# Two weight sums of each FFN tile made by an adding DMA, and a new order of some FFN products

## The chip, the cores and the metric

The program runs on one core of one Trainium2 chip. The metric is device time in microseconds (us), lower is better; three runs of the kernel before gave 568.59, 568.89 and 569.35 us, so the time before is their median, 568.89 us.

## What is computed

One decoder layer over 512 tokens of width 1024 in float32: a norm, a mixer (attention, a state-space group, pooling), an output projection with a residual add, a norm, a SwiGLU FFN with 2816 hidden units, a residual add and a final norm. The change lies in the FFN:

```python
    x = x + jnp.concatenate([y_attn, y_ssd, y_pool], axis=-1) @ w_out
    h = rmsnorm(x, norm_ffn)
    gate, up = jnp.split(h @ w_gate_up, 2, axis=-1)
    return x + (jax.nn.silu(gate) * up) @ w_down
```

## The kernel before

Every float32 product is made of three matmuls: weights and activations are split into a high part in fp32r (a copy on ACT) and a low part (a subtraction on DVE), and `mm3` (L184) multiplies high by high, low by high and high by low.

The hidden units of the FFN are cut into 22 tiles of 128, in the groups `GROUPS` = (0, 4), (4, 8), (8, 12), (12, 16), (16, 18), (18, 22). Tile 0 (`PLAIN`) is multiplied plainly. For each of the other 21 tiles, gate and up of that tile are a 2 by 2 block product: two halves of the inner dimension (g1, g2 of the gate weights; v1, v2 of the up weights, 512 columns each in a tile of 128 x 1024) by two halves of the tokens (256 each). It is done with seven products instead of eight, P1 to P7, each of 4 x 3 matmuls of 256 columns. P1 and P2 take g1 and g2, P4 takes v2; P5, P6, P7 and P3 take the weight sums s1 = v1 + v2, s2 = s1 + g1, s3 = g1 + v1 and s4 = s2 + g2. P4 to P7 multiply sums of the activations, T1 to T4, which DVE makes once at the start of the FFN (`h2_sums`). P1, P6, P7 and P4 follow one another in one PSUM bank, `psB`; ACT copies its running value to a tile `u` after P1, P6 and P7 (L1107), before the next product may add to it. P5 and P3 share `psC`, P2 has `psA`.

The weights come by `load_ahead` (L879): a list of 512 KB loads on SP's queue into `NRAW` = 4 buffers; r_g is a tile's gate, r_u its up, r_d a piece of w_down. The work on them is a list of steps per tile, `plan`: `split_g`, `add_up` (all four sums, on DVE, into two tiles `sa`, `sb` with two buffers in all), `split_v`, and `split_s` twice, for sa = (s1, s2) and for sb = (s3, s4). A step is taken by `advance` whenever buffers of the split weights are free and its load should have landed, in the course of the products; a scheduler then fixes each engine's order. An engine takes its instructions in that order, and waits at the first whose operands are not there.

`pair_order` writes down the products of a group: two tiles overlap, so that PE has other work while ACT copies `psB`. The last two products of a group's last tile, P4 and P3, are its tail; they stand behind the first block of the group's down products (`pd`), four banks of 512 tokens each, added by DVE to the residual x1 (`add_x1`, L797). The tiles 1 to 3 (`EARLY`) have P1 and P2 ahead of all (`FIRST`), since the sums T come late. At that time, the start of the FFN, the loads of x1, of the gate weights of tiles 1 to 3 and the last split of w_out (half of it on GpSimd, POOL in the profile) fall together.

```python
            s_, q_ = sums[i] = [sp.tile([P, 1024], F32, name=f"{n}{i}", tag="s") for n in ("sa", "sb")]
            nc.vector.tensor_tensor(s_[:, :512], v1, v2, ALU.add)
            nc.vector.tensor_tensor(s_[:, 512:], s_[:, :512], g1, ALU.add)
            nc.vector.tensor_tensor(q_[:, :512], g1, v1, ALU.add)
            nc.vector.tensor_tensor(q_[:, 512:], s_[:, 512:], g2, ALU.add)
```

Of the kernel before, what the change touches and what calls it, by code (L numbers as in the profile page):

```python
# [114 lines left out]

def layer(tc, xT, xn, w1, wz, wv, wo, wgu, wd, par, poolw, gffn, gfin, out):
    nc = tc.nc
    L = Lanes()
    ctx = ExitStack()
    with ctx:  # L120
# [740 lines left out]
        def all_loads():  # L861
            for lo_, hi_ in GROUPS:
                order = [(w, i) for i in range(lo_, hi_) for w in "gu"]
                if lo_ == 0:
                    first = [(w, i) for i in PLAIN for w in "gu"] + [("g", i) for i in EARLY]
                    order = first + [q for q in order if q not in first]
                for w, i in order:
                    yield (w, i), wgu[2 * i + (w == "u")]
                for h in range(2):
                    for kp in range(lo_ // 2, hi_ // 2):  # L870
                        yield ("d", kp, h), wd[2 * kp + h]

# [6 lines left out]
        def load_ahead():  # L879
            while len(raws) < NRAW:  # L880
                key, src = next(loads, (None, None))
                if key is None:
                    return
                raws[key] = rawp.tile([P, 1024], F32, name="r_" + "_".join(map(str, key)), tag="raw")
                nc.sync.dma_start(raws[key], src)
                dma_free[0] = max(dma_free[0], L.clock) + 1.6
                landed[key] = dma_free[0] + 2.5

        def used(*keys):
            for key in keys:  # L890
# [12 lines left out]
        def add_up(i):  # L903
            load_ahead()
            r0, r1 = raws["g", i], raws["u", i]
            g1, g2, v1, v2 = r0[:, :512], r0[:, 512:], r1[:, :512], r1[:, 512:]
            s_, q_ = sums[i] = [sp.tile([P, 1024], F32, name=f"{n}{i}", tag="s") for n in ("sa", "sb")]
            nc.vector.tensor_tensor(s_[:, :512], v1, v2, ALU.add)
            nc.vector.tensor_tensor(s_[:, 512:], s_[:, :512], g1, ALU.add)  # L909
            nc.vector.tensor_tensor(q_[:, :512], g1, v1, ALU.add)  # L910
            nc.vector.tensor_tensor(q_[:, 512:], s_[:, 512:], g2, ALU.add)
            used(("g", i))

# [13 lines left out]
        def split_s(i, m):  # L927
            kind = ("wx", "w")[m]
            h_, l_ = slot(kind, f"sh{m}{i}"), slot(kind, f"sl{m}{i}")
            hi_lo(sums[i][m], h_, l_, nc.vector)  # L930
            for k_, n in enumerate(((5, 6), (7, 3))[m]):
                ops[i, n] = (h_[:, k_ * 512 : (k_ + 1) * 512], l_[:, k_ * 512 : (k_ + 1) * 512])

        def split_d(kp, h):
# [194 lines left out]
        def block(i, n):  # L1129
# [9 lines left out]
            for kt in range(4):  # L1139
                sl = slice(kt * P, (kt + 1) * P)  # L1140
                mm3(ps, w_hi[:, sl], w_lo[:, sl], *moving(n, kt), new and kt == 0, kt == 3, chain=not new)
            if n in (2, 5, 3):
                done("w" if n == 3 else "wx", 2)
            elif n == 4:
                done("wx", 1)
# [34 lines left out]
        def pair_order(lo_, hi_):  # L1180


            tiles = [i for i in range(lo_, hi_) if i not in PLAIN]
            order = []
            for i, nxt in zip(tiles, tiles[1:] + [None]):
                if (i, 6) not in order:
                    order += [(i, n) for n in (1, 2, 6, 5, 7) if (i, n) not in order and (i, n) not in FIRST]
                if nxt is None:
                    return order, [(i, 4), (i, 3)]
                if nxt in EARLY:  # L1190
                    order += [(nxt, 6), (i, 4), (nxt, 5), (i, 3), (nxt, 7)]
                else:
                    order += [(nxt, 1), (i, 4), (nxt, 2), (i, 3)]

        for gi, (lo_, hi_) in enumerate(GROUPS):
# [21 lines left out]
            for h in range(2):  # L1217
                last = gi == len(GROUPS) - 1 and h == 1
                kps = range(lo_ // 2, hi_ // 2)
                if not last:  # L1220
                    pss = [bank(f"pd{gi}{h}_{t}") for t in range(NT)]
                    for kp in kps:
                        w_hi, w_lo = need(("d", kp, h))
                        for j in range(2):
                            k = 2 * kp + j
                            js = slice(j * 512, (j + 1) * 512)
                            if h == 0 and k == lo_ + 1:
                                for q in tail:
                                    block(*q)
                            for t in range(NT):  # L1230
                                ts_ = slice(t * P, (t + 1) * P)
                                pd_end = mm3(pss[t], aT[k][0][:, ts_], aT[k][1][:, ts_], w_hi[:, js], w_lo[:, js], k == lo_, k == hi_ - 1)
                            advance()
# [52 lines left out]
def pack(inputs):  # L1286
# [64 lines left out]
```

## Time and profile before

| what | value |
|---|---|
| median of 3 runs | 568.89 us |
| the profiled execution, its own time | 569.56 us |
| its span | 567.9 us |
| PE matmuls | 556.4 us, 3504 of them |
| DVE, ACT, POOL busy | 432.2, 308.1, 30.7 us |
| moved by DMA | 61.62 MB, 109 GB/s on the mean |
| mean granted PE clock | 0.994 of full speed |

The span runs from the first to the last instruction; the execution's own time is 1.7 us longer. The FFN begins at about 213 us; the last of the output projection, the loads of x1 and the norm lie before it. In the rows below, PE is the matmul engine, SPq is SP's queue of DMA issues, and what stands in brackets behind a row is how long its engine stood idle before it and what ended that.

### The profile page before, as it was taken

How to read it: one execution, taken by the hardware profiler on the slowest of the kernel's cores; microseconds unless marked ns; L12 is line 12 of the kernel's file. 1: busy time of each engine (PE TensorE's matmuls, PEld its weight loads, DVE VectorE, ACT ScalarE, POOL GpSimd, SP SyncE). 2: the span in 40 equal slices, each digit the busy share in tenths (PEclk: the TensorE clock that was granted, in tenths of full speed). 3: DMA queues.
4: the chain of work that ended last, by engine and by line, in shares of the span. 5: the costliest groups of instructions: out<-in, count | busy, mean ns of one | idle time of the engine just before them, and what ended most of it. 6: DMA issues, size and time to landing. Idle time of an engine off the chain costs nothing.

```text
span 567.9 us, 9056 instructions
## 1 busy us (share of the span) xinstructions
PE 556.4 (98%) x3504; PEld 504.2 (89%) x3504; DVE 432.2 (76%) x788; ACT 308.1 (54%) x561; POOL 30.7 (5%) x47
## 2 busy tenths in 40 slices
PE   8999999999999999999999999999999999999995
PEld 4998998888987889998899989998999889899984
DVE  4479866898999678999967777776867876787346
ACT  5687645777767456655264524543255425345344
POOL 6001002006110000000000000000000000000000
PEclk8999999999999999999999999999999999999998
DMA  7962233322213601255232332343043233222004
GB/s 239 316 193 82 75 111 112 131 76 86 82 39 117 254 1 38 78 186 183 74 119 107 112 111 75 112 122 139 19 164 105 86 101 122 76 75 75 1 0 148
DMA packets 19663, 61.62 MB, mean 109 GB/s; under 512 B 2316, under 2 KB 3748, under 8 KB 19620
## 3 DMA queue, kind: packets, MB, share of 16 engines
q1 hardware_dynamic: 19044, 60.00, 31.3%
q10 hardware_dynamic: 576, 1.05, 0.5%
q8 instruction: 27, 0.44, 0.3%
q14 instruction: 16, 0.13, 0.1%
HBM read 58.93 MB, written 2.11 MB: 107 GB/s over the span
## 4 chain that ended last, share of the span: by engine, by line
PE 92%; DVE 4%; ACT 2%; DMA 1%; issue 1%; SPq 0%; ACTq 0%; DVEq 0%
PE psB L186 7%; PE psB L188 7%; PE psB L187 7%; PE pd L186 6%; PE pd L187 6%; PE pd L188 6%; PE pc L186 4%; PE pc L188 4%; PE pc L187 4%; PE psC L187 3%; PE psC L188 3%; PE psC L186 3%; PE po L186 2%; PE po L188 2%; PE po L187 2%; PE pn L186 2%
## 5 line engine op out<-in xcount | busy, mean ns | idle before, releaser
L187 PE MATMUL pd<-dl,aTh 128*128 128x512 f32 x160 | 62.4, 390 | 0.0
L186 PE MATMUL pd<-dh,aTh 128*128 128x512 f32 x160 | 61.6, 391 | 0.0
L188 PE MATMUL pd<-dh,aTl 128*128 128x512 f32 x160 | 58.6, 390 | 0.0
L157 DVE TENSOR_TENSOR wlo<-raw,whi 128x1024 fp32r<-128x1024 f32 (+3 forms) x29 | 34.3, 1181 | 14.3 <-ACT whi L156 13.1
L156 ACT ACTIVATE whi<-raw 128x1024 fp32r<-128x1024 f32 (+3 forms) x34 | 31.5, 930 | 23.5 <-PE pc L187 11.6
L858 ACT ACTIVATE sh<-sb 128x1024 fp32r<-128x1024 f32 x21 | 22.2, 1059 | 39.5 <-PE pd L187 18.5
L186 PE MATMUL pc<-hT_hi,whi 128*128 128x512 f32 x104 | 41.7, 401 | 0.0
L188 PE MATMUL pc<-hT_hi,wlo 128*128 128x512 f32 x104 | 40.8, 393 | 0.0
L1107 ACT COPY u<-psB 128x256 f32<-128x256 f32 x63 | 23.1, 366 | 32.6 <-PE psB L188 31.7
L187 PE MATMUL pc<-hT_lo,whi 128*128 128x512 f32 x104 | 40.7, 392 | 0.0
L858 ACT ACTIVATE dh<-r_d 128x1024 fp32r<-128x1024 f32 x22 | 23.3, 1060 | 26.3 <-PE psC L187 12.8
L859 DVE TENSOR_TENSOR gl<-r_g,gh 128x1024 fp32r<-128x1024 f32 x22 | 26.9, 1224 | 12.8 <-ACT gh L858 7.0
L186 PEld LDWEIGHTS pd<-dh,aTh 128*128 128x128 f32 x160 | 30.0, 188 | 6.2 <-ACT aTh L858 0.4
L188 PEld LDWEIGHTS pd<-dh,aTl 128*128 128x128 f32 x160 | 30.1, 188 | 6.1
L187 PEld LDWEIGHTS pd<-dl,aTh 128*128 128x128 f32 x160 | 30.1, 188 | 6.0
L859 DVE TENSOR_TENSOR sl<-sa,sh 128x1024 fp32r<-128x1024 f32 x21 | 25.7, 1223 | 11.6 <-PE psA L187 10.4
L858 ACT ACTIVATE gh<-r_g 128x1024 fp32r<-128x1024 f32 x22 | 23.3, 1058 | 20.0 <-DMA r_g<-wgu 10.8
L859 DVE TENSOR_TENSOR sl<-sb,sh 128x1024 fp32r<-128x1024 f32 x21 | 25.6, 1220 | 10.5 <-ACT sh L858 7.3
L859 DVE TENSOR_TENSOR dl<-r_d,dh 128x1024 fp32r<-128x1024 f32 x22 | 26.9, 1222 | 4.8 <-ACT dh L858 4.7
L797 DVE TENSOR_TENSOR x<-pd,x 128x512 f32<-128x512 f32 x44 | 27.9, 684 | 3.0 <-PE pd L188 3.0
L858 ACT ACTIVATE sh<-sa 128x1024 fp32r<-128x1024 f32 x21 | 22.3, 1060 | 14.3 <-DVE sa L909 7.9
L186 PE MATMUL po<-whi,mixT_hi 128*128 128x512 f32 x64 | 25.5, 401 | 0.0
(321 smaller groups left out, 1840.4 us busy)
## 6 DMA issues: line engine op xcount, KB each, us to landing
r_g<-wgu SPq DMA_DIRECT2D x22, 512.0 KB, 3.5
r_u<-wgu SPq DMA_DIRECT2D x22, 512.0 KB, 3.8
r_d<-wd SPq DMA_DIRECT2D x22, 512.0 KB, 3.6
raw<-w SPq DMA_DIRECT2D x13, 512.0 KB, 3.3
raw<-wo SPq DMA_DIRECT2D x8, 512.0 KB, 3.2
rawx<-xT SPq DMA_DIRECT2D x8, 256.0 KB, 3.4
rawn<-xn SPq DMA_DIRECT2D x4, 512.0 KB, 4.6
x<-xn SPq DMA_DIRECT2D x4, 512.0 KB, 7.3
```

Of the source, the lines that this page charges most:

```text
L156: nc.scalar.activation(hi[:, sl], raw[:, sl], AF.Copy)
L157: eng.tensor_tensor(lo[:, sl], raw[:, sl], hi[:, sl].bitcast(F32), ALU.subtract)
L186: nc.tensor.matmul(ps, s_hi, m_hi, start=first, stop=False, skip_group_check=chain)
L187: nc.tensor.matmul(ps, s_hi, m_lo, start=False, stop=False, skip_group_check=chain)
L188: last_mm = nc.tensor.matmul(ps, s_lo, m_hi, start=False, stop=last, skip_group_check=chain)
L797: nc.vector.tensor_tensor(x1[t][:, cs], ps, x1[t][:, cs], ALU.add)
L858: nc.scalar.activation(hi, src, AF.Copy)
L859: eng.tensor_tensor(lo, src, hi.bitcast(F32), ALU.subtract)
L1107: nc.scalar.copy(u_, e["B"])
```

## The change

The host packs a further array `wgs`: for each tile (v2, g1) and (v1, v1). SP loads the first into a tile `sa`; then GpSimd sends a DMA that adds the second to it on the way. So `sa` comes out as (s1, s3) with no DVE work. The two adds that are left, s2 and s4, are written over r_g's two halves, so r_g is kept until its second split. r_u loads only v2 (256 KB) where it was 512 KB. The two buffers of `sa` are asked for two tiles ahead: `sum_ahead` is called twice at the start and then after each split of an `sa`. P5 and P7 now have one split and P6 and P3 the other, and `pair_order` puts P5 ahead of P6. For the fifth group the tail is gone: P4 and P3 of tile 17 stand among P1 and P2 of tile 18. Where a group has a tail, its first down products are held until the last tile's latest product is issued.

```diff
@@ load_ahead, all_loads
                 for w, i in order:
-                    yield (w, i), wgu[2 * i + (w == "u")]
+                    half = w == "u" and i not in PLAIN
+                    yield (w, i), wgu[2 * i + (w == "u")][:, 512 * half :], 512 * half
...
-                nc.sync.dma_start(raws[key], src)
+                nc.sync.dma_start(raws[key][:, c0:], src)
...
+        sum_order = [i for i in range(FT) if i not in PLAIN]
+
+        def sum_ahead():
+
+            if sum_order:
+                i = sum_order.pop(0)
+                t_ = sums[i, 0] = sp.tile([P, 1024], F32, name=f"sa{i}", tag="sa")
+                nc.sync.dma_start(t_, wgs[2 * i])
+                nc.gpsimd.dma_start(t_, wgs[2 * i + 1], accum_op=ALU.add)
...
         def add_up(i):
             load_ahead()
-            r0, r1 = raws["g", i], raws["u", i]
-            g1, g2, v1, v2 = r0[:, :512], r0[:, 512:], r1[:, :512], r1[:, 512:]
-            s_, q_ = sums[i] = [sp.tile([P, 1024], F32, name=f"{n}{i}", tag="s") for n in ("sa", "sb")]
-            nc.vector.tensor_tensor(s_[:, :512], v1, v2, ALU.add)
-            nc.vector.tensor_tensor(s_[:, 512:], s_[:, :512], g1, ALU.add)
-            nc.vector.tensor_tensor(q_[:, :512], g1, v1, ALU.add)
-            nc.vector.tensor_tensor(q_[:, 512:], s_[:, 512:], g2, ALU.add)
-            used(("g", i))
+            r0, sa = raws["g", i], sums[i, 0]
+            sums[i, 1] = r0
+            nc.vector.tensor_tensor(r0[:, :512], sa[:, :512], r0[:, :512], ALU.add)
+            nc.vector.tensor_tensor(r0[:, 512:], r0[:, :512], r0[:, 512:], ALU.add)
...
-            hi_lo(sums[i][m], h_, l_, nc.vector)
-            for k_, n in enumerate(((5, 6), (7, 3))[m]):
+            hi_lo(sums.pop((i, m)), h_, l_, nc.vector)
+            for k_, n in enumerate(((5, 7), (6, 3))[m]):
                 ops[i, n] = (h_[:, k_ * 512 : (k_ + 1) * 512], l_[:, k_ * 512 : (k_ + 1) * 512])
+            if m == 0:
+                sum_ahead()
+            else:
+                used(("g", i))
...
         crit = []
+        for _ in range(2):
+            sum_ahead()
...
@@ block
-            if n in (2, 5, 3):
+            if n in (2, 7, 3):
                 done("w" if n == 3 else "wx", 2)
...
@@ pair_order
-                if (i, 6) not in order:
-                    order += [(i, n) for n in (1, 2, 6, 5, 7) if (i, n) not in order and (i, n) not in FIRST]
+                if (i, 5) not in order:
+                    order += [(i, n) for n in (1, 2, 5, 6, 7) if (i, n) not in order and (i, n) not in FIRST and (n > 2 or i not in st)]
+                if nxt is None and hi_ == 18:
+
+                    return order + [(hi_, 1), (i, 4), (hi_, 2), (i, 3)], []
                 if nxt is None:
                     return order, [(i, 4), (i, 3)]
                 if nxt in EARLY:
-                    order += [(nxt, 6), (i, 4), (nxt, 5), (i, 3), (nxt, 7)]
+                    order += [(nxt, 5), (i, 4), (nxt, 6), (i, 3), (nxt, 7)]
...
+                            hold = tc.issue_after(st[hi_ - 1]["end"]) if tail and h == 0 and k == lo_ else nullcontext()
+                            with hold:
+                                for t in range(NT):
+                                    ts_ = slice(t * P, (t + 1) * P)
+                                    pd_end = mm3(pss[t], aT[k][0][:, ts_], aT[k][1][:, ts_], w_hi[:, js], w_lo[:, js], k == lo_, k == hi_ - 1)
...
@@ pack
+    g_, v_ = wgu[0::2], wgu[1::2]
+    wgs = np.concatenate([v_[:, :, 512:], g_[:, :, :512], v_[:, :, :512], v_[:, :, :512]], axis=2)
+    wgs = np.ascontiguousarray(wgs.reshape(FT, P, 2, 1024).transpose(0, 2, 1, 3)).reshape(2 * FT, P, 1024)
```

How the instructions move is shown at three places. In the names the number behind a letter is the tile of the FFN, and the last four digits are a buffer's running number.

SP's queue at the start of the FFN, behind the loads of x1, before:

```order
L785 DMA x1_2_2050<-xn 128x1024
L785 DMA x1_3_2051<-xn 128x1024
L885 DMA r_g_1_2112<-wgu 128x1024
L885 DMA r_g_2_2114<-wgu 128x1024
L885 DMA r_g_3_2160<-wgu 128x1024
L885 DMA r_u_1_2172<-wgu 128x1024
L1241 DMA gf_5962<-gfin 128x1024
L885 DMA r_u_2_2610<-wgu 128x1024
L885 DMA r_u_3_2615<-wgu 128x1024
```

and now:

```order
L785 DMA x1_2_2050<-xn 128x1024
L785 DMA x1_3_2051<-xn 128x1024
L903 DMA sa1_2073<-wgs 128x1024
L903 DMA sa2_2076<-wgs 128x1024
L886 DMA r_g_1_2118<-wgu 128x1024
L886 DMA r_g_2_2120<-wgu 128x1024
L886 DMA r_g_3_2166<-wgu 128x1024
L886 DMA r_u_1_2178<-wgu 128x512
L1258 DMA gf_5941<-gfin 128x1024
L886 DMA r_u_2_2615<-wgu 128x512
L903 DMA sa3_2621<-wgs 128x1024
L886 DMA r_u_3_2641<-wgu 128x512
```

The loads of sa1 and sa2 have come in between x1 and the gates of tiles 1 to 3, and the one of sa3 between r_u of tiles 2 and 3. On POOL, the last instructions before (the split of w_out, `wlo30`, is the last but the end of the program):

```order
L703 MEMSET pwa1_1701 128x16
L703 MEMSET pwb1_1702 128x16
L487 TENSOR_TENSOR sz_219<-skp_238,sz_219 128x384 x2
L157 TENSOR_TENSOR wlo30_2093<-raw30_2091,whi30_2092 128x512
L1347 UNCONDITIONAL_BRANCH
L1347 ISA
```

and now, with the same split in the middle:

```order
L703 MEMSET pwb1_1702 128x16
L487 TENSOR_TENSOR sz_219<-skp_238,sz_219 128x384 x2
L904 DMA sa1_2073<-wgs 128x1024
L904 DMA sa2_2076<-wgs 128x1024
L157 TENSOR_TENSOR wlo30_2099<-raw30_2097,whi30_2098 128x512
L904 DMA sa3_2621<-wgs 128x1024
```

The adding DMAs of sa1 and sa2 stand ahead of `wlo30`, whose tile PE reads in the last products of the output projection. On DVE, the sums and splits of tile 1 (sh/sl are the high and low part of a pair of weight sums, the 0 or 1 ahead of the tile's number saying which split) before:

```order
L1024 TENSOR_TENSOR T1l_2322<-h2f10_2263,T1h_2321 128x4x128
L908 TENSOR_TENSOR sa1_2604<-r_u_1_2172 128x512
L910 TENSOR_TENSOR sb1_2605<-r_g_1_2112,r_u_1_2172 128x512
L859 TENSOR_TENSOR vh1_2612<-r_u_1_2172,vh1_2612 128x512
L1028 SCALAR_TENSOR_TENSOR h2f31_2431<-h2f10_2263,h2f31_2431 128x512
L1024 TENSOR_TENSOR T3l_2326<-h2f30_2422,T3h_2325 128x4x128
L909 TENSOR_TENSOR sa1_2604<-sa1_2604,r_g_1_2112 128x512
L1099 TENSOR_TENSOR g3_2541<-psA_3_2528,u1_3_2526 128x256
L1030 SCALAR_TENSOR_TENSOR h2f11_2272<-h2f31_2431,h2f11_2272 128x512
L1024 TENSOR_TENSOR T2l_2324<-h2f31_2431,T2h_2323 128x4x128
L911 TENSOR_TENSOR sb1_2605<-sa1_2604,r_g_1_2112 128x512
```

and now:

```order
L1036 TENSOR_TENSOR T1l_2328<-h2f10_2269,T1h_2327 128x4x128
L917 TENSOR_TENSOR r_g_1_2118<-sa1_2073,r_g_1_2118 128x512
L859 TENSOR_TENSOR vh1_2612<-r_u_1_2178,vh1_2612 128x512
L859 TENSOR_TENSOR sl01_2618<-sa1_2073,sh01_2617 128x1024
L917 TENSOR_TENSOR r_g_2_2120<-sa2_2076,r_g_2_2120 128x512
L1040 SCALAR_TENSOR_TENSOR h2f31_2437<-h2f10_2269,h2f31_2437 128x512
L1036 TENSOR_TENSOR T3l_2332<-h2f30_2428,T3h_2331 128x4x128
L918 TENSOR_TENSOR r_g_1_2118<-r_g_1_2118 128x512
```

The low part of tile 1's first split, `sl01`, stands three places behind T1's low part (T1l), where before ten instructions stood between them. On PE, the end of P7 of tile 17 (T3) and the start of its P4 (T4) before:

```order
L186 MATMUL psB_17_5176<-T3h_2325,sh117_5029 128x256
L187 MATMUL psB_17_5176<-T3l_2326,sh117_5029 128x256
L188 MATMUL psB_17_5176<-T3h_2325,sl117_5030 128x256
L186 MATMUL psB_17_5176<-T4h_2327,vh17_5003 128x256
L187 MATMUL psB_17_5176<-T4l_2328,vh17_5003 128x256
L188 MATMUL psB_17_5176<-T4h_2327,vh17_5003 128x256
```

and now the same end of P7:

```order
L186 MATMUL psB_17_5159<-T3h_2331,sh017_4993 128x256
L187 MATMUL psB_17_5159<-T3l_2332,sh017_4993 128x256
L188 MATMUL psB_17_5159<-T3h_2331,sl017_4994 128x256
L186 MATMUL psB_18_5290<-h2_hi_2079,gh18_5105 128x256
L187 MATMUL psB_18_5290<-h2_lo_2080,gh18_5105 128x256
L188 MATMUL psB_18_5290<-h2_hi_2079,gl18_5106 128x256
L186 MATMUL psB_18_5290<-h2_hi_2079,gh18_5105 128x256
```

P4 of tile 17 comes 21 matmuls later now, after the rest of P1 and all of P2 of tile 18.

## Rows read from the trace of the kernel before

**Rows 1.** Page, part 1: busy us of each engine, share of the span, instructions.

```profile
PE 556.4 (98%) x3504; PEld 504.2 (89%) x3504; DVE 432.2 (76%) x788; ACT 308.1 (54%) x561; POOL 30.7 (5%) x47
```

**Rows 2.** Windows: length, then PE, PEld, DVE, ACT, POOL busy; PEclk, DMA share, GB/s.

```profile
220.00:240.00 20.00, 19.93 (x167) 19.68 (x165) 19.41 (x32) 14.33 (x27) 0.00 (x0) 1.00 0.21 73
...
240.00:260.00 20.00, 19.24 (x140) 18.27 (x141) 19.08 (x29) 12.10 (x19) 0.00 (x0) 1.00 0.56 183
260.00:480.00 220.00, 220.00 (x1511) 205.63 (x1510) 166.95 (x246) 101.02 (x155) 0.00 (x0) 1.00 0.33 108
480.00:500.00 20.00, 19.36 (x117) 16.93 (x116) 15.37 (x25) 6.95 (x10) 0.00 (x0) 1.00 0.15 54
```

**Rows 3.** Timeline of PE, 235 to 249 us: start, length, instruction, idle before.

```profile
235.35 0.28 PE L186 MATMUL psB<-T2h,sh 128*128 128x256 f32 x1
...
239.53 0.28 PE L187 MATMUL psB<-T3l,sh 128*128 128x256 f32 x1
239.65 0.28 PE L188 MATMUL psB<-T3h,sl 128*128 128x256 f32 x1
240.76 0.39 PE L186 MATMUL psB<-T2h,sh 128*128 128x256 f32 x1 [0.83 <-ACT sh L858]
...
248.42 0.28 PE L187 MATMUL psC<-T1l,sh 128*128 128x256 f32 x1
248.69 0.39 PE L186 MATMUL psB<-T4h,vh 128*128 128x256 f32 x1
```

**Rows 4.** Timeline of PE, 483 to 499 us.

```profile
483.71 0.28 PE L188 MATMUL psB<-T3h,sl 128*128 128x256 f32 x1
484.45 0.39 PE L186 MATMUL psB<-T4h,vh 128*128 128x256 f32 x1 [0.46 <-ACT u L1107]
...
496.53 1.98 PE L188 MATMUL pd<-dh,aTl 128*128 128x512 f32 x8
498.68 0.39 PE L186 MATMUL psB<-h_hi,gh 128*128 128x256 f32 x1 [0.18 <-DVE x L797]
```

**Rows 5.** Timeline of DVE, 227 to 235 us; last, the groups of instructions of ACT.

```profile
227.93 0.69 DVE L908 TENSOR_TENSOR sa<-r_u 128x512 f32<-128x512 f32 x1
...
234.25 1.23 DVE L859 TENSOR_TENSOR sl<-sa,sh 128x1024 fp32r<-128x1024 f32 x1 [0.49 <-ACT sh L858]
...
L858 ACT ACTIVATE sh<-sa 128x1024 fp32r<-128x1024 f32 x21 | 22.3, 1060 | 14.3 <-DVE sa L909 7.9 <-PE psB L188 6.4
```

**Rows 6.** DMA issues: xcount, KB, median us to landing; last, tile x, 176 to 200 us.

```profile
r_g<-wgu SPq DMA_DIRECT2D x22, 512.0 KB, 3.5
out<-x SPq DMA_DIRECT2D x2, 128.0 KB, 2.0
...
DMA to landing us min/median/max: 6.0/7.3/9.8
```

**Rows 7.** Start of the FFN, 183 to 207 us: windows, queue of SP, DMA issue, POOL, PE, DVE.

```profile
184.00:186.00 2.00, 2.00 (x10) 1.67 (x9) 0.97 (x2) 0.60 (x1) 0.00 (x0) 1.00 1.04 424
...
183.24 3.75 SPq L885 DMA_DIRECT2D r_g<-wgu  x3
...
r_g<-wgu SPq DMA_DIRECT2D x1, 512.0 KB, 7.5
...
193.91 1.29 POOL L157 TENSOR_TENSOR wlo<-raw,whi 128x512 fp32r<-128x512 f32 x1 [25.49 <-ACT whi L156]
...
198.98 0.39 PE L187 MATMUL po<-wlo,mixT_hi 128*128 128x512 f32 x1
...
199.63 0.69 DVE L797 TENSOR_TENSOR x<-po,x 128x512 f32<-128x512 f32 x1 [1.41 <-PE po L188]
204.70 2.73 DVE L994 SCALAR_TENSOR_TENSOR xh<-x,rsay,gn 128x512 f32<-128x512 f32 x4
...
206.01 2.14 PE L1001 MATMUL ps_h<-ident,xh 128*128 128x128 f32 x16
```

More of the change, by code (lines that the diff above doesn't have):

```diff
@@ L12 @@
-from contextlib import ExitStack
+from contextlib import ExitStack, nullcontext
 import numpy as np
@@ L113, in drain, with layer @@
             self.tick(0.5)
-def layer(tc, xT, xn, w1, wz, wv, wo, wgu, wd, par, poolw, gffn, gfin, out):
+def layer(tc, xT, xn, w1, wz, wv, wo, wgu, wgs, wd, par, poolw, gffn, gfin, out):
     nc = tc.nc
@@ L867, in all_loads @@
                 for w, i in order:
-                    yield (w, i), wgu[2 * i + (w == "u")]
+                    half = w == "u" and i not in PLAIN
+                    yield (w, i), wgu[2 * i + (w == "u")][:, 512 * half :], 512 * half
                 for h in range(2):
                     for kp in range(lo_ // 2, hi_ // 2):
-                        yield ("d", kp, h), wd[2 * kp + h]
+                        yield ("d", kp, h), wd[2 * kp + h], 0
         loads = all_loads()
@@ L880, in load_ahead @@
             while len(raws) < NRAW:
-                key, src = next(loads, (None, None))
+                key, src, c0 = next(loads, (None, None, None))
                 if key is None:
@@ L1140, in block @@
                 sl = slice(kt * P, (kt + 1) * P)
-                mm3(ps, w_hi[:, sl], w_lo[:, sl], *moving(n, kt), new and kt == 0, kt == 3, chain=not new)
-            if n in (2, 5, 3):
+                e["end"] = mm3(ps, w_hi[:, sl], w_lo[:, sl], *moving(n, kt), new and kt == 0, kt == 3, chain=not new)
+            if n in (2, 7, 3):
                 done("w" if n == 3 else "wx", 2)
@@ L1229, in layer @@
                                     block(*q)
-                            for t in range(NT):
-                                ts_ = slice(t * P, (t + 1) * P)
-                                pd_end = mm3(pss[t], aT[k][0][:, ts_], aT[k][1][:, ts_], w_hi[:, js], w_lo[:, js], k == lo_, k == hi_ - 1)
+                            hold = tc.issue_after(st[hi_ - 1]["end"]) if tail and h == 0 and k == lo_ else nullcontext()
[3 more added lines that the diff above has]
+                                    pd_end = mm3(pss[t], aT[k][0][:, ts_], aT[k][1][:, ts_], w_hi[:, js], w_lo[:, js], k == lo_, k == hi_ - 1)
                             advance()
@@ L1330, in pack @@
     return dict(
-        xT=xT, xn=x.reshape(NT, P, D), w1=w1, wz=wz, wv=wv, wo=wo, wgu=wgu, wd=wdn, par=par, poolw=poolw,
+        xT=xT, xn=x.reshape(NT, P, D), w1=w1, wz=wz, wv=wv, wo=wo, wgu=wgu, wgs=wgs, wd=wdn, par=par, poolw=poolw,
         gffn=f["norm_ffn"][0:1], gfin=f["norm_final"][None, :],
```

## Prediction

> **What bounds the kernel now.** The profiled execution took 569.56 us with a span of 567.9 us, 0.67 us above the median of 568.89 us; the sum below is made against the former and carried over to the latter. I read the engine totals first: PE is busy for 556.4 us, 98% of the span, and DVE for 432.2 us [rows 1]. So only what PE stands still for can be won, as its matmuls stay as many and as wide. The stretches say where that is: from 260 to 480 us PE reads 220.00 of 220, while from 240 to 260 and from 480 to 500 it misses 0.76 and 0.64 us [rows 2]. What else PE idles lies in the mixer and at the two ends of the program, where the change touches nothing. Third, the PE rows around those two places. A 256-column matmul follows the one before after 0.12 us but its row is 0.28 us long, so a gap hides its first 0.16 us, and the row after a gap is 0.39 instead of 0.28 us, 0.11 us of restart. At 239.65 the next row should stand at 239.77 and stands at 240.76, released by a split on ACT: 0.99 + 0.11 us. At 248.42 it is 0.15 + 0.11 us [rows 3]. **First place: 1.36 us.** At 483.71 P4 of tile 17 waits for the copy of P7's sum to `u`, 0.62 + 0.11 us; at 496.53 eight matmuls of 0.227 us end at 498.35 and tile 18's first starts at 498.68 once DVE has freed a bank: 0.33 + 0.11 us [rows 4]. **Second place: 1.17 us.** Together 2.53 us, 0.44% of the time, is all the change can win.
>
> **The sums off DVE.** Two of four adds go for 21 tiles: 42 instructions of 0.69 us [rows 5], 29 us of DVE time. Where PE reads full that is worth nothing: DVE was not waited for there (166.95 of 220 us busy [rows 2]). It counts in the first place, where DVE is busy 19.08 of 20 us [rows 2]. There tile 1's first sum started at 227.93 and the low half of its split only at 234.25, after five additions and the T sums between [rows 5]. Now that split needs no add: by the DVE order above it comes third after T1's low half, behind an add and a 512-column split, so it ends at 227.93 + 0.69 + 0.69 + 1.23 = 230.5 us, some 5 us before PE asks for it at 235.35 [rows 3, 5]. P5, which needs only s1 and the early T1, is now PE's first. The wait of 239.65 goes, and the one of 248.42, which stood behind the same DVE chain: -1.36 us. **What is late next is tile 3.** Its `sa` reuses tile 1's buffer: the plain load can start at 230.5, takes 3.5 us as the other loads of 512 KB do [rows 6], and at 234.0 GpSimd may send the adding DMA. PE reaches P5 of tile 3 after 38 matmuls of 0.12 us from 235.35, at 239.9; the ACT split before it takes 1.06 us [rows 5], so `sa3` must have landed by 238.8: **the adding DMA may take 4.8 us**. No row shows one. From below it is a plain load, 3.5 us; from above the 9.8 us that a load took while the DMA engines were full [rows 6]. I take 5.5 us, nearest to the plain load: 128 KB land in 2.0 and 512 KB in 3.5 us [rows 6], so 512 KB more to move cost 2.0 us, and an adding DMA fetches the destination too. That is 0.7 us late plus 0.1 us of restart: +0.8 us (0 to 5.1). The Trainium skill ("DMA: Bandwidth & Descriptors", Anatomy of one DMA — SWDGE (gpsimd) path) gives about 2.0 us plus bytes over 436 GB/s for a GpSimd DMA; as an estimate, with the bytes counted twice, that is 4.4 us, by which nothing would wait and the sum below would be -2.3 us. No run here shows it yet.
>
> **Adding DMAs in the steady stretch.** A tile's buffer is asked for two tiles ahead, and a tile is 84 matmuls of 0.12 us and 24 of 0.227 us, some 15 us of PE. Plain load and adding DMA are 3.5 + 5.5 = 9 us, so one tile of cover is enough; only above about 12 us for the adding DMA alone would it be gone. In SP's queue the `sa` load waits for a DVE split, and r_u and r_g stand behind it; r_u of tile 3 waits for the split of v2 of tile 2 in any case. A tile moves 768 KB more, 16.5 MB in all, onto DMA engines that are busy a third of the time [rows 2]. I cost this at nothing.
>
> **The start of the FFN.** Here the two first `sa` loads go in front of the three r_g loads in SP's queue, and the two adding DMAs in front of the last split of w_out on POOL (orders above). From 184 to 186 us the engines already move 424 GB/s, and the third r_g, issued at 183.24 + 3.75 - 0.33 = 186.66, lands 7.5 us later, at 194.2 [rows 7]. Two plain loads ahead cost 1.05 MB / 0.424 = 2.5 us: 196.7. Its split on ACT and DVE, 1.06 + 1.23 us [rows 5], ends at 199.0, ahead of the DVE add at 199.63 that stands behind it [rows 7]: nothing. If all of the adding DMAs' traffic, 2.1 MB with both passes, went ahead as well, it would be 4.9 us more and the add 4.3 us late; the transposes at 206.01 have 0.6 us of slack, as the first of the four normalised halves is ready at 204.70 + 0.7 [rows 7], so PE would lose 3.7 us. An adding DMA can only be sent when its plain load has landed, with little of the r_g traffic left, so I take +0.2 us (0 to 3.7). On POOL the split ran at 193.91 for 1.29 us and PE reads its result at 198.98 [rows 7]; two issues between SP's 0.33 us and 1.29 us each from about 193 still let it end by 197: nothing, unless one issue takes over 2 us.
>
> **P5 ahead of P6** moves little by itself: the PE order before already mixed both, since P6 waits for a copy. **Tile 17's P4 and P3 among tile 18's products**: the copy that P4 waits for now runs under 21 matmuls of tile 18, and tile 18's start no longer waits for banks behind the eight matmuls: -1.17 us. The cover is gone only if tile 18's sums were late; their buffer is free a tile and a half before. The hold on the first down matmul only fixes an order on PE.
>
> **Sum**: -1.36 - 1.17 + 0.8 + 0.2 = -1.5 us: 568.0 us for the profiled execution, **567.4 us** for the median. About 0.2% (1.1 us) is what a measurement of this kernel can tell from no change, so the forecast lies little beyond it.
>
> **Rivals.** (1) *Slower: the adding DMA takes 9 to 10 us.* At 235 to 245 us PE then stands for `sa3`: 9.8 - 4.8 + 0.1 = 5.1 us instead of 0.8, and the time is 568.9 - 2.53 + 0.2 + 5.1 = 571.7. The saving is gone where the adding DMA takes 7.0 us, and the kernel is slower by over 0.2% from 8.2 us. For it: 9.8 us has been seen for a plain load [rows 6]. Against: that was with the engines full, and around 240 us they are busy a fifth to a half of the time [rows 2]. Chance 0.18. (2) *No change: the start loses what the sums win.* The adding DMAs sit in another queue than the r_g loads; if the engines serve both in turn while they are full, the last two r_g loads, 1.05 MB, take 2.5 us more; the third lands at 199.2, its split ends at 201.5, the add is 1.9 us late, and PE stands for 1.3 us at the transposes: 567.4 - 0.2 + 1.3 = 568.5. For it: the engines are full there [rows 7]. Against: the plain loads land late in that burst. The Trainium skill has this rule (same page, Queues, rings and completion order): each DMA engine takes its queues in turn, packet by packet. By that rule the third r_g would wait so; no row of this trace has two busy queues. Chance 0.2. (3) *The first place doesn't give way.* If the T sums and tile 2's splits, not the adds, hold DVE's chain, the stall comes back behind P6 and only the second place is won, less 0.2: 568.89 - 1.17 + 0.2 = 567.9, within 0.2%. For it: DVE stays full there. Against: P5 gets ready 5 us early. Chance 0.1.
>
> **Numbers.** The forecast has 0.5; its own range is 566.4 (sum of -2.5) to 567.7. Rival 1 reaches to 571.7, rival 2 to 569. The range of 566.3 to 571.0 leaves out the far end of rival 1. Faster by over 0.2%: 0.5; within 0.2%: rivals 2 and 3, 0.3; slower: rival 1 and a late POOL split, 0.2.
>
> **What would show it.** Right: no PE row with an idle bracket between 235 and 262 us longer than 0.7 us, and that one at tile 3's P5 behind its ACT split; none from 480 to 500; landings of the adding DMA near 5.5 us; DVE busy near 404 us. Wrong: an ACT split of `sa3` that waits over 2 us for a DMA (rival 1), a gap at the 16 transposes near 206 us (rival 2), or gaps of PE between 260 and 480 us, where I expect none: that would say that the steady stretch is not covered.

## The result and the profile after

The changed kernel takes 572.42 us, median of 4 runs (572.15 to 574.26), beside 569.06 us of the kernel before (4 runs): ratio 1.0067, 95% interval 1.0044 to 1.0089. It is slower by 3.4 us, where 1.5 us less had been forecast, and lies above the range of 566.3 to 571.0. The profiled execution took 572.63 us, 3.07 us more than that of before.

The page, parts 1 and 3 (busy us of each engine; DMA queue: packets, MB, share of 16 engines):

```profile
PE 556.6 (97%) x3504; PEld 505.7 (89%) x3504; DVE 408.2 (72%) x746; ACT 304.9 (53%) x561; POOL 49.1 (9%) x68
...
q1 hardware_dynamic: 22068, 65.50, 34.2%
q0 software_dynamic: 3024, 11.01, 11.4%
```

DVE is 24 us less busy than in [rows 1], where 29 had been forecast from rows of 0.69 us (they start only about 0.6 us apart, as at 227.19, 227.79 and 228.40 us), and PE has the same work. The 21 adding DMAs are the queue q0. They hold 11.4% of 16 engines over 570.9 us: **3.1 us of all 16 DMA engines for each**. The windows (length, then PE, PEld, DVE, ACT, POOL busy; PEclk, DMA share, GB/s) say where PE lost time:

```profile
220.00:240.00 20.00, 19.68 (x165) 19.47 (x163) 17.87 (x29) 15.00 (x27) 0.88 (x1) 1.00 0.36 92
240.00:260.00 20.00, 17.22 (x125) 16.96 (x126) 13.46 (x20) 9.75 (x17) 1.75 (x2) 0.91 0.87 253
...
260.00:480.00 220.00, 220.00 (x1497) 205.03 (x1496) 150.32 (x217) 97.54 (x154) 12.15 (x14) 1.00 0.57 155
...
480.00:500.00 20.00, 20.00 (x150) 19.13 (x149) 14.59 (x22) 9.81 (x18) 1.73 (x2) 1.00 0.60 158
520.00:540.00 20.00, 19.48 (x159) 19.11 (x158) 10.82 (x19) 8.19 (x16) 0.00 (x0) 1.00 0.17 53
```

Beside [rows 2]: the steady stretch is full as before, and 480 to 500 us has become full, so the second place is won. But 220 to 260 us misses 3.1 us instead of 0.8, with a granted clock of 0.91 on the mean from 240 us on, and 520 to 540 us misses 0.5 us that it didn't miss before. The timeline of PE shows both (start, length, instruction, idle before):

```profile
239.40 0.28 PE L188 MATMUL psB<-T2h,sl 128*128 128x256 f32 x1
242.78 0.56 PE L186 MATMUL psC<-T1h,sh 128*128 128x256 f32 x1 [3.11 <-ACT sh L858]
243.14 0.42 PE L187 MATMUL psC<-T1l,sh 128*128 128x256 f32 x1
243.36 0.41 PE L186 MATMUL psB<-T3h,sh 128*128 128x256 f32 x1
...
246.31 0.27 PE L187 MATMUL psB<-T2l,sh 128*128 128x256 f32 x1
246.43 0.28 PE L188 MATMUL psB<-T2h,sl 128*128 128x256 f32 x1
...
536.70 0.28 PE L188 MATMUL psB<-T2h,sl 128*128 128x256 f32 x1
537.49 0.39 PE L186 MATMUL psB<-T3h,sh 128*128 128x256 f32 x1 [0.52 <-ACT u L1119]
```

The first is tile 3's P5, just where the forecast had put the new stall, but 3.26 us long instead of 0.7. Behind it PE runs at half clock (the rows are 0.41 us long and 0.21 us apart instead of 0.28 and 0.12; 243 to 246 us was granted 0.50 of full speed, 1.2 GHz). From 239.40 to 246.43 are 18 row spacings, 2.16 us at 0.12 us; they took 7.03: **4.87 us lost, 3.26 of waiting and 1.6 of restart and slow clock**. The second is the last tile's P7, 0.67 + 0.10 us behind P6. The stalls of [rows 3] and [rows 4] are all gone. Together: 4.87 + 0.77 - 1.36 - 1.17 = +3.11 us, against 3.07 measured. (Outside these places two smaller differences nearly cancel: the transposes ahead of the FFN start at 205.61 instead of 206.01 us [rows 7], and from the start of the last matmul to the end of the span are 6.92 instead of 6.67 us.)

Who was late for tile 3, from the timelines of SP, POOL, ACT and DVE:

```profile
230.29 0.33 SPq L903 DMA_DIRECT2D sa<-wgs  x1
234.79 0.33 SPq L886 DMA_DIRECT2D r_u<-wgu  x1
235.92 0.33 SPq L903 DMA_DIRECT2D sa<-wgs  x1
237.66 6.80 SPq L886 DMA_DIRECT2D r_d<-wd  x3
...
234.38 0.88 POOL L904 DMA_DIRECT2D sa<-wgs  x1 [38.97 <-ACT T2h L1035]
...
238.55 0.63 ACT L858 ACTIVATE vh<-r_u 128x512 fp32r<-128x512 f32 x1 [1.56 <-DMA r_u<-wgu]
241.67 1.06 ACT L858 ACTIVATE sh<-sa 128x1024 fp32r<-128x1024 f32 x1 [2.50 <-DMA sa<-wgs]
...
229.00 1.22 DVE L859 TENSOR_TENSOR sl<-sa,sh 128x1024 fp32r<-128x1024 f32 x1
```

Tile 1's split ends at 230.2 (229.00 + 1.22), and `sa3`'s plain load goes out at once. It lands after 3.5 us, at 233.8, but GpSimd sends the adding DMA only at 234.38: 0.6 us from the landing to the issue, as for all 19 sums behind the first two (0.58 to 0.72 us). The adding DMA lands at 241.67, **7.3 us later**. SP had meanwhile sent r_u of tile 3, `sa4` and the first r_d, all within 3.3 us. The groups of DMA issues (KB, median us to landing) over the whole program, over those sent from 230.2 to 231 us, and from 232.5 to 241 us:

```profile
sa<-wgs SPq DMA_DIRECT2D x21, 512.0 KB, 4.5
sa<-wgs POOLq DMA_DIRECT2D x21, 512.0 KB, 5.5
...
sa<-wgs SPq DMA_DIRECT2D x1, 512.0 KB, 3.5
...
sa<-wgs POOLq DMA_DIRECT2D x1, 512.0 KB, 7.3
sa<-wgs SPq DMA_DIRECT2D x1, 512.0 KB, 6.7
```

The median is the 5.5 us that was estimated. Eleven of the 21 take 5.2 to 5.5 us, and the timelines of SP and POOL show that none of these has a load of SP sent from 1.1 us ahead of it to 1.6 us behind it. Eight take 6.2 to 8.3 us, and each of them has one sent within 0.9 us of it. (The other two, 6.7 and 8.7 us, are those of the burst at the start.) The last one of the program has nothing but an r_u of 256 KB near it, and takes 7.1 us:

```profile
496.58 0.86 POOL L904 DMA_DIRECT2D sa<-wgs  x1 [9.75 <-DMA sa<-wgs]
497.06 0.33 SPq L886 DMA_DIRECT2D r_u<-wgu  x1
...
sa<-wgs POOLq DMA_DIRECT2D x1, 512.0 KB, 7.1
```

Part of the delay lies ahead of the transfer: queue q0 shows no packet of `sa3`'s adding DMA for 2.7 us after it was sent, where the one at 333.73 us, with nothing sent near it, shows its first after 1.6 us.

### The profile page after: what moved, and what is told of

Same layout as the page of the kernel before. It is cut to its first block, busy times and chain, and to the rows that moved or that the text cites. A ratio compares the mean times of both kernels' runs of the same rounds, so it can differ in the third digit from the quotient of the medians.

```text
span 570.9 us, 9133 instructions
## 1 busy us (share of the span) xinstructions
PE 556.6 (97%) x3504; PEld 505.7 (89%) x3504; DVE 408.2 (72%) x746; ACT 304.9 (53%) x561; POOL 49.1 (9%) x68
## 3 DMA queue, kind: packets, MB, share of 16 engines
q0 software_dynamic: 3024, 11.01, 11.4%
## 4 chain that ended last, share of the span: by engine, by line
PE 89%; DVE 4%; ACT 3%; DMA 2%; issue 1%; SPq 0%; ACTq 0%
PE psB L186 7%; PE psB L188 7%; PE psB L187 7%; PE pd L186 6%; PE pd L187 6%; PE pd L188 6%; PE pc L186 4%; PE pc L188 4%; PE pc L187 4%; PE psC L186 3%; PE psC L187 3%; PE psC L188 3%; PE po L186 2%; PE po L187 2%; PE po L188 2%; PE pn L186 2%
## 5 line engine op out<-in xcount | busy, mean ns | idle before, releaser
L904 POOL DMA_DIRECT2D sa<-wgs x21 | 18.4, 876 | 309.7 <-DVE gl L859 77.8
L157 DVE TENSOR_TENSOR wlo<-raw,whi 128x1024 fp32r<-128x1024 f32 (+3 forms) x29 | 33.1, 1143 | 15.1 <-ACT whi L156 15.0
L858 ACT ACTIVATE sh<-r_g 128x1024 fp32r<-128x1024 f32 x21 | 22.2, 1056 | 29.5 <-PE pd L187 18.4
L859 DVE TENSOR_TENSOR sl<-r_g,sh 128x1024 fp32r<-128x1024 f32 x21 | 25.6, 1221 | 8.5 <-ACT sh L858 8.5
L186 PE MATMUL psC<-T1h,sh 128*128 128x256 f32 x84 | 24.0, 286 | 3.1 <-ACT sh L858 3.1
```

The costliest lines, as they stand in the source:

```text
L157: eng.tensor_tensor(lo[:, sl], raw[:, sl], hi[:, sl].bitcast(F32), ALU.subtract)
L186: nc.tensor.matmul(ps, s_hi, m_hi, start=first, stop=False, skip_group_check=chain)
L858: nc.scalar.activation(hi, src, AF.Copy)
L859: eng.tensor_tensor(lo, src, hi.bitcast(F32), ALU.subtract)
L904: nc.gpsimd.dma_start(t_, wgs[2 * i + 1], accum_op=ALU.add)
```

## The experiments

The theory at this point (A): the loss is `sa3` alone, with the clock's fall behind it, and 0.77 us at the last tile; the second place is a real gain. The rivals: adding DMAs cost PE in many places (B); the 7.3 us is the chain's own length whatever lies beside it (C). Each run has a ratio to the kernel before on the same chip, with its 95% interval; 0.1% is 0.57 us.

**The fifth group's order alone**, on the kernel before, and the changed kernel without it.

```diff
--- e4: in pair_order of the kernel before
...
+                if nxt is None and hi_ == 18:
+                    return order + [(hi_, 1), (i, 4), (hi_, 2), (i, 3)], []
--- e5: the same two lines taken out of the changed kernel
```

> The kernel before with nothing but the fifth group's last two products put among tile 18's first; the sums stay on DVE, the order P6, P5 stays. Theory A: the second place goes (1.17 us), the first place stays at 1.36 us: 569.06 - 1.17 = 567.9 us. Rival: the wait comes back at another row of the same stretch, 569.0 us.

> The changed kernel without the edit of the fifth group's order. Theory A: the second place stands as before the change, 1.17 us more than the changed kernel, 573.6 us. Rival: with 29 us of adds off DVE the banks are freed earlier and the second place is gone without the edit, 572.4 us.

Measured: alone 567.08 us beside 568.18, ratio 0.9978 (0.9968 to 0.9987), 1.2 us less; PE reads 20.00 of 20 from 480 to 500 us and still has 1.00 + 0.10 us at 237.8 us. The step was right. Without it the changed kernel takes 574.14 us, ratio 1.0104 (1.0088 to 1.0119). The lighter DVE didn't free the second place, on the contrary. Its waits of PE from 480 to 500 us (in total, times, longest):

```profile
PE psB L186 <- ACT u L1119: 0.9, 1, 0.9
PE pd L186 <- ACT aTh L858: 0.6, 1, 0.6
```

**A third buffer**, so that `sa3` needn't wait for tile 1.

```diff
-        sp = fpool("sums", 2)
+        sp = fpool("sums", 3)
...
-        for _ in range(2):
+        for _ in range(3):
             sum_ahead()
```

The lines left out make the room: among them, `a` has one buffer instead of two, and no run shows what that alone costs.

> Three buffers for sa instead of two and three sums asked for at the start, so that tile 3's no longer waits for tile 1's buffer. (The room comes from the squares' throw-away tiles, which now lie in the h2f tiles, and from one buffer less for a.) Theory A, the loss is sa3 alone (stall 3.26 us, restart 0.24 us, 15 matmuls at half clock 1.41 us = 4.9 us): the gap near 239 us goes and the time is 572.4 - 4.9 = 567.5 us, up to 568.5 us if a third plain and a third adding DMA in the burst at 181 to 201 us hold up the r_g loads there by 1 us. Theory B, the adding DMAs cost PE in many small places: the gap goes, but the time stays at 571 us or above.

Measured: 574.36 us beside 568.18, ratio 1.0112 (1.0092 to 1.0131): worse than the changed kernel, and as a test of A against B it failed, since it made waits of its own. The waits of PE from 186 to 262 us, and one of ACT at the start:

```profile
PE psC L186 <- ACT sh L858: 3.0, 1, 3.0
PE ps_h L1013 <- DVE xh L1006: 1.4, 1, 1.4
PE psB L186 <- ACT sh L858: 0.6, 2, 0.4
...
ACT gh L858 <- DMA r_g<-wgu: 4.7, 3, 2.3
```

The 1.4 us at the transposes near 206 us is rival 2's mechanism: with three sums in the burst the r_g loads come so late that their splits hold up the norm on DVE. And `sa3`, now landed long before, was split no sooner: ACT takes its work in order, and ahead of that split stands the split of v2 of tile 3, whose r_u was sent at 239.82 and landed at 245.0. That split would have to be watched in the other runs too.

**What lies beside the adding DMA.** Three edits meant to take loads away from it.

```diff
--- e3: the first group's r_d loads go out behind sa5's load
...
+                with tc.issue_after(sent[5]) if key[:2] == ("d", 0) else nullcontext():
+                    nc.sync.dma_start(raws[key][:, c0:], src)
...
--- e9: as e3, and sa4's load is asked for at tile 3's split
+                for _ in range({2: 0, 3: 2}.get(i, 1)):
+                    sum_ahead()
...
--- e11: as e3, and tile 4 makes s1 and s3 on DVE
...
+            if i == 4:
+                nc.vector.tensor_tensor(sa[:, :512], r1[:, :512], r1[:, 512:], ALU.add)
+                nc.vector.tensor_tensor(sa[:, 512:], r0[:, :512], r1[:, :512], ALU.add)
...
```

> The four r_d loads of the first group are issued behind tile 5's sa load in SP's queue, that is after sa3 has been split, and so no longer lie beside sa3's adding DMA. Theory A (the adding DMA took 7.3 us there because it shared the DMA engines with r_d): it takes about 5.4 us, its median, the stall falls from 3.1 to 1.2 us, and the time is 572.4 - 1.9 = 570.5 us, or 569.1 us if the clock then doesn't fall either. Theory C (7.3 us is what the chain takes here whatever else runs): stall of 3.1 us and 572.4 us as before.

> As the kernel with the later r_d loads, and tile 4's sa load, too, goes out only when sa3 has been split; beside sa3's adding DMA lies r_u of tile 3 alone (256 KB). Theory A2 (the DMA that shared the engines with it was not r_d but sa4's plain load, which SP sends 1.5 us behind): the adding DMA lands in 5.4 to 6.1 us, PE stands 1.2 to 1.9 us instead of 3.1, and the time is 1.2 to 3.3 us below the changed kernel's. Theory C (7.3 us whatever else runs): the stall stays at 3.1 us.

> In the last two tries sa4's plain load (sent 1.6 us behind sa3's adding DMA) still lay beside it. Here tile 4 makes its sums on DVE, tile 5's sa load takes the buffer that sa3 leaves, and the r_d loads stand behind it in SP's queue: beside sa3's adding DMA lies only r_u of tile 3 (256 KB). Theory A2 (it shares the engines): it lands 5.2 to 6.1 us after its issue, PE stands 1.0 to 1.9 us at tile 3's P5 instead of 3.1, and the clock stays at 1.00 behind it. Theory C (7.3 us whatever else runs): 7.3 us and 3.1 us. The time of the whole is not what is asked, since later loads are later, too.

Measured: ratios 1.0063 (1.0048 to 1.0078), 1.0073 (1.0053 to 1.0092) and 1.0052 (1.0035 to 1.0069); the adding DMA took 7.3, 6.8 and 6.3 us, PE stood 3.03, 2.76 and 2.58 us. e3 did what it said: SP sent its first r_d at 245.01 us, after `sa3` had landed, and the adding DMA took 7.3 us all the same. So r_d is not what made it late. e9 and e11 did not do what they said. As in e3, SP sent a plain `sa` load 1.4 to 1.8 us behind the adding DMA: moved back in the program, it had nothing to wait for in the queue, so it went out as soon as its buffer was free (tile 4's in e9, tile 5's in e11). Beside the adding DMA e9 thus has the same loads as e3, and the 6.8 and 7.3 us show how far two like cases lie apart. In e11 the first r_d came too, at 237.52 us, and r_u had become the late one: ACT's split of v2 waited for it 3.5 us, until 240.48. e9's time also holds a new stall of PE, 0.95 us at 252.31 us behind ACT, which had waited for the later r_d.

**Only three tiles by DMA, then nothing but r_u beside.** The first takes the later `sa` loads away altogether; the second also makes SP wait.

```diff
--- e15
-        sum_order = [i for i in range(FT) if i not in PLAIN]
+        sum_order = [1, 2, 3]
...
+            if (i, 0) not in sums:
+                nc.vector.tensor_tensor(s_[:, :512], r1[:, :512], r1[:, 512:], ALU.add)
+                nc.vector.tensor_tensor(s_[:, 512:], r0[:, :512], r1[:, :512], ALU.add)
--- e16: as e15, and ahead of the first group's r_d loads in SP's queue
+            if (i, m) == (3, 0):
+                sent.append(nc.sync.dma_start(mark_, h_[:1, :16].bitcast(F32)).ins)
...
```

> The changed kernel with adding DMAs for tiles 1 to 3 alone; tiles 4 to 21 make their sums on DVE, so that no further sa load is sent behind sa3's. Beside sa3's adding DMA lie r_u of tile 3 (256 KB) and, from 3.3 us after it on, the first r_d load. Theory A2 (the 7.3 us is shared engines): it lands 5.2 to 6.2 us after its issue, tile 3's P5 stands 0.9 to 2.0 us instead of 3.1, and the clock stays at 1.00. Theory C (the second leg of the chain takes 7.3 us here whatever is beside it): 7.3 us and 3.1 us.

> As the kernel with three tiles by DMA, but the r_d loads wait in SP's queue behind a DMA of 64 bytes that reads the split of sa3, so that they can't start before sa3 has landed; beside sa3's adding DMA lies only r_u of tile 3 (256 KB). Theory A2 (shared engines): it lands 5.4 + 0.75 = 6.1 us or less after its issue instead of 6.9, and PE stands 1.9 us instead of 2.7. Theory C: 6.9 us and 2.7 us stay.

Measured: e15 ratio 1.0043 (1.0030 to 1.0057), adding DMA 6.9 us, stall 2.71; r_d had moved up to 236.43 when `sa4` went. e16 ratio 1.0056 (1.0036 to 1.0076). Its DMA views from 232 to 246 us and its PE row:

```profile
q0 software_dynamic: 144, 0.52, 22.8%
...
sa<-wgs POOLq DMA_DIRECT2D x1, 512.0 KB, 6.6
...
241.32 0.39 PE L186 MATMUL psC<-T1h,sh 128*128 128x256 f32 x1 [2.69 <-ACT sh L858]
```

With r_u of 256 KB alone beside it the DMA still took 6.6 us, not the 6.1 expected: it was sent 0.5 us later (0.2 us of that is a shift of the whole trace) and PE stood as long. The result lies between the theories: C's 2.7 us of standing came, and the DMA took 0.3 us less than C's 6.9 us and 0.5 us more than A2's 6.1. Without `sa4` and r_d beside it, it took 0.7 us less than in the changed kernel, little more than the 0.5 us between e3 and e9, so a share of theirs isn't shown. One adding DMA holds all 16 engines for 0.228 x 14 = 3.2 us here. What stands above 5.5 us, 1.1 us, has only r_u left to explain it, and no run was made without r_u. The last tile's sum, at 491 to 499 us, speaks for r_u: in the changed kernel, e3, e9, e11 and e13 SP sent r_u 0.4 to 0.6 us behind the adding DMA, which took 6.5 to 7.1 us; in e5 and e6 r_u had gone out 0.54 and 0.78 us ahead of it, and it took 5.2. This sorts what happened, it is no experiment, and single adding DMAs were long with nothing sent that near (7.0 us at 332.84 us in e5). The cause of this part is argued, not shown.

**Copying instead of adding**, with the number, size and order of the DMAs as they were. `sa` then holds the second operand; the kernel leaves out the sums s1 and s3, and only its time is of use.

```diff
-                nc.gpsimd.dma_start(t_, wgs[2 * i + 1], accum_op=ALU.add)
+                nc.gpsimd.dma_start(t_, wgs[2 * i + 1])
```

> GpSimd's DMA copies instead of adding, so that sa holds the second operand and not the sum; the number, size and order of the DMAs and all waits stay. Theory A (an adding DMA keeps the engines busy for twice as long, 3.1 us where a plain one of 512 KB takes 1.5 us, and that is why sa3 is late): sa3 lands 1.6 us sooner, 5.7 us after its issue, PE stands 1.5 us instead of 3.1 us, and the time is 1.6 to 3 us below the changed kernel's (the upper end if the clock then doesn't fall). Rival D (what costs is GpSimd's way of issuing and the second leg of the chain, not the adding): 7.3 us and 3.1 us stay.

Measured: 568.64 us, ratio 1.0006 (0.9991 to 1.0022), 3.5 us below the changed kernel by the ratios, a little over the upper end. From its page, the groups of DMA issues over the whole program and from 232.5 us, and the timelines of ACT and PE:

```profile
q0 software_dynamic: 3024, 11.01, 5.5%
...
sa<-wgs POOLq DMA_DIRECT2D x21, 512.0 KB, 3.5
sa<-wgs POOLq DMA_DIRECT2D x1, 512.0 KB, 3.5
...
237.92 0.63 ACT L858 ACTIVATE vh<-r_u 128x512 fp32r<-128x512 f32 x1 [2.02 <-DMA r_u<-wgu]
238.46 1.04 ACT L858 ACTIVATE sh<-sa 128x1024 fp32r<-128x1024 f32 x1
...
239.55 0.39 PE L186 MATMUL psC<-T1h,sh 128*128 128x256 f32 x1 [1.03 <-ACT sh L858]
```

With r_u, `sa4` and r_d sent behind it as before, the copying DMA lands in 3.5 us, where 5.7 had been expected, and holds the engines for 0.055 x 566.1 / 21 = 1.5 us, half of the adding one's 3.1. **The adding is what costs: 3.8 us of landing at this place.** Of these, 2.0 us lie between the two medians, 5.5 and 3.5 us; the other 1.8 us are what the adding one takes here above its own median. D falls. The clock stayed at 1.00 here. And there was a second wait under the first: `sa3` landed at 236.5, yet its split began only at 238.46, behind v2's split on ACT, which waited for r_u. PE stood 1.03 us all the same. As long as r_u lands as it did here, no speed of the adding DMA makes the stall less than that; no run moved r_u, or put `sa3`'s split ahead of v2's.

**Who needs the adding DMA.** Tiles 1 and 2 only (e10); all but tile 3 (e13); none at all (e12), each with P6 ahead of P5 again in tile 21 (e6 is that alone, on the changed kernel); and e10 with the old order of P5 and P6 from tile 4 on (e14).

```diff
--- e6, and within e10, e12, e13
+                    ... for n in ((1, 2, 6, 5, 7) if nxt is None and hi_ == FT else (1, 2, 5, 6, 7)) ...
+            with tc.issue_after(e["end"]) if (i, n) == (FT - 1, 5) else nullcontext():
...
--- e10, e14: with e15's adds on DVE, as e12 and e13
+        sum_order = [1, 2]
--- e13
+        sum_order = [i for i in range(FT) if i not in PLAIN and i != 3]
...
--- e12
+        sum_order = []
--- e14: in place of e6's edit
+                    ... for n in ((1, 2, 5, 6, 7) if i in EARLY else (1, 2, 6, 5, 7)) ...
```

> In tile 21 alone P6 stands ahead of P5 again, with P5 held behind P6's last matmul, so that P5's twelve matmuls lie between P6 and P7. Theory A (the new gap at 536.7 us, 0.67 + 0.10 us, is P7 waiting for the copy of P6's sum, since P5 no longer stands between them): the gap goes, and the time is 0.8 us below the changed kernel's, some 0.5% over the kernel before instead of 0.67%. Rival (an engine is late there, whatever the order): another gap of about that size near 536 us and no change.

> Only tiles 1 and 2 get their sums from the adding DMA, in the burst at the start, where no buffer has to come free first; tiles 3 to 21 make all four sums on DVE again (r_u loaded whole). P5 ahead of P6 and the fifth group's order stay, and P6 stands ahead of P5 in tile 21. Theory A (what the change wins is DVE time before 235 us and the second place; what it loses is the chain of two DMAs for sa3): DVE has four adds less ahead of tile 3 and PE doesn't wait near 239 us by more than 0.5 us; both places are won: 2.0 to 2.5 us below the kernel before, ratio 0.996. Rival: tile 3's two adds more, in the stretch where DVE is full, bring back a stall of about 1 us at 240 us: ratio 0.998, as with the fifth group's order alone.

> As the kernel with two tiles by DMA, but tiles 4 to 21 have their sums from adding DMAs again; tile 3 alone makes them on DVE. Theory A (the whole loss is sa3, and adding DMAs cost nothing from 260 us on): the same time as with two tiles by DMA, ratio 0.9966. Theory B (they cost in the steady stretch): slower than that by 0.5 us or more.

> The two orders of the change (P5 ahead of P6, with P6 first in tile 21; the fifth group's last two products among tile 18's first) without any adding DMA: DVE makes all four sums in all tiles. Theory A (tiles 1 and 2 need the DVE time for the first place): tile 1's split is 1.4 to 2.8 us later than with two tiles' sums by DMA, a stall of 0.5 to 1.4 us stands again near 240 us, and the ratio is 0.998. Rival E (P5 first is enough, as it needs s1 and T1 only): no stall there, ratio 0.9965, and the DMA sums are worth nothing anywhere.

> As the kernel with two tiles by DMA, but P5 goes ahead of P6 in tiles 1 to 3 alone; from tile 4 on the order is P6, P5, P7 as before the change, without the hold in tile 21. If the 0.33 us gap near 544 us is the hold's, it goes: 0.2 to 0.4 us below that kernel; otherwise the same.

| run | adding DMAs for | median, us | before, us | ratio (95%) |
|---|---|---|---|---|
| changed kernel | 1 to 21 | 572.42 | 569.06 | 1.0067 (1.0044 to 1.0089) |
| e6 | 1 to 21 | 571.62 | 568.24 | 1.0056 (1.0040 to 1.0072) |
| e10 | 1, 2 | 566.62 | 568.24 | 0.9966 (0.9953 to 0.9979) |
| e14 | 1, 2 | 566.61 | 568.22 | 0.9968 (0.9955 to 0.9982) |
| e13 | all but 3 | 566.85 | 568.22 | 0.9971 (0.9958 to 0.9984) |
| e12 | none | 568.55 | 568.22 | 1.0004 (0.9993 to 1.0015) |

e13 is the test that the third buffer had failed to be: 18 adding DMAs more than e10 and the same time within the intervals. Its windows:

```profile
240.00:260.00 20.00, 20.00 (x145) 18.92 (x144) 17.44 (x27) 12.00 (x20) 1.76 (x2) 1.00 0.87 254
260.00:480.00 220.00, 220.00 (x1517) 205.92 (x1517) 147.35 (x212) 96.99 (x153) 12.15 (x14) 1.00 0.55 156
```

So the loss at the first place is `sa3` alone, and B falls. The adding DMAs win nothing in the steady stretch either. Between e12 and e10 lies what two of them are worth at the first place, 0.38% or 2.2 us; the waits of PE from 230 to 262 us without them (with them the trace shows none):

```profile
PE psB L188 <- DVE sl L859: 0.7, 1, 0.7
PE psC L186 <- ACT sh L858: 0.4, 1, 0.4
PE psC L188 <- DVE sl L859: 0.3, 1, 0.3
```

E falls: P5 first is not enough by itself. A's ratio for e12, 0.998, was missed by 0.24%, 1.4 us: PE loses 2.1 us in four gaps from 235 to 243 us, not 0.5 to 1.4 us in one. e10's 0.34% is a little under the 2.0 to 2.5 us that were expected. e6's gap at 536.7 us is gone from the trace, with 0.23 us come back at 549 us and a longer stall at `sa3` in the profiled execution (3.45 us); its time alone can't be told from the changed kernel's. e14 shows no difference to e10; only the 0.33 us gap near 544 us went, and another of 0.21 us stands at 532 us. **e10 and e14 beat both kernels**, by 0.34% and 0.32% against the one before, 1.9 and 1.8 us of the 2.53 us that there were to win; e13 does, too, by 0.29%.

## Why the prediction was wrong

- **The first place gives way: right.** Tile 1's split was done at 230.2 (forecast 230.5), both old stalls went, -1.36 us. Rival 3 falls.
- **The second place: right.** -1.17 us by the trace; 1.2 us measured alone.
- **Tile 3's sum, +0.8 us: the step that failed**, right in place and mechanism, mis-sized in three ways. It measured 4.87 us. (1) "I take 5.5 us": with little beside it an adding DMA does take 5.2 to 5.5 us, but here it took 7.3, +1.8 us. I had costed the extra traffic at nothing from the mean share of the engines over 20 us and more, and had not listed which loads SP sends in those very microseconds: r_u, `sa4` and r_d. Taking r_d away changed nothing (e3), and the traces point at r_u, but which of them it is stays open. The 5.5 us itself is the measured median, and adding takes the 2.0 us more than copying that I had added; part of that is luck, since those 2.0 us came from setting a store of 128 KB against a load of 512 KB [rows 6]. (2) "May take 4.8 us": it was sent at 234.38, not 234.0, since 0.6 us pass from the landing of the plain load to GpSimd's issue, which the sum had put at nothing (the load itself was sent 0.2 us sooner than forecast and took its 3.5 us); and PE stood at the row after 239.40, where 239.9 had been counted; with 1.1 us for the split, 4.05 us were left, +0.75 us. (3) "0.1 us of restart": 1.6 us, because the clock fell after the stall; the stalls of the FFN before, of 0.83 us at most, had not shown that, and the bound didn't allow for it. With the 0.7 us late of the forecast: 1.8 + 0.75 + 0.7 + 1.6 = 4.85. A fourth, hidden beneath: r_u of tile 3, in front of `sa3` on ACT, sets a floor of about 1 us (e8). I had named that load as waiting "in any case" and not followed it to ACT.
- **The start of the FFN, +0.2 us: nothing.** ACT took up the third r_g at 196.46 us (it had been forecast to land at 196.7), DVE's part of its split ended at 198.79, ahead of the add at 199.00, and the 16 transposes near 206 us are spaced as before. Rival 2 falls. The mechanism is real, though: one sum more there costs 1.4 us (e2).
- **The steady stretch at nothing: right**, though the adding DMAs, of 3.1 us each, and the plain loads ahead of them raise the share of busy engines there from 0.33 to 0.57.
- **P5 ahead of P6 "moves little": wrong for the last tile.** In the others, products of a neighbouring tile stand between P6 and P7. Tile 21 has no next tile, and the wait of P7 for the copy of P6's sum costs 0.77 us.
- **Rival 1** was the right one at the wrong price: slower by the adding DMA from 8.2 us on, I said; it was slower at 7.3 us, since neither the clock, nor the 0.75 us of (2), nor the last tile was in that sum. The Trainium skill ("DMA: Bandwidth & Descriptors", Anatomy of one DMA — SWDGE (gpsimd) path) had given 4.4 us with the bytes counted twice; the trace's shortest is 5.2, and the copying DMA's 3.5 us is nearer to its 2.0 us plus bytes over 436 GB/s (3.2 us as an estimate).

## What to carry to other kernels

A sum made by an adding DMA frees the engine that added, but puts two transfers in series behind a buffer, and 0.6 us between them. It pays where the buffer is free long before (tiles 1 and 2 here, 2.2 us) and loses at the first reuse that is tight. Price such a chain by the loads that its neighbours in the queues send in those same microseconds, and follow each of them to the in-order engine that takes it. When products are reordered, look at the last tile, which has no successor to fill its gaps.

## What the runs showed of the hardware

- An adding DMA of 512 KB holds the 16 DMA engines for 3.1 us, a copying one from the same queue for 1.5 us. The adding one lands in 5.2 to 5.5 us where SP sends no load near it (eleven of the changed kernel's 21), in 6.2 to 8.3 us where it sends one within 0.9 us (eight); GpSimd begins to issue it 0.58 to 0.72 us after the landing that it waits for, and is busy for 0.87 us with it, 0.53 us with the copying one.
- After PE stalls of 2.6 to 3.5 us at this place the granted clock went from 1.00 to 0.50 (2.4 to 1.2 GHz) in eight of nine profiled executions, for 12 to 29 matmul rows that took 0.09 us more each; after 2.76 us in e9, and after the 0.83 and 1.03 us of the kernel before and of e8, it stayed.
